# Moving three bias-broadcast DMAs from SyncE's queue to ScalarE's queue

## The chip, the cores and the metric

The kernel runs on one core of one Trainium2 chip. The metric is the device time of one execution in microseconds; the median of the timed executions counts. Times inside the kernel come from one profiled execution and are counted from the start of its span.

## What is computed

The program is one layer of a hybrid decoder for 2048 tokens of width 1024. Half of the heads run a recurrent mixer (RWKV-7), the other half attend over three dilated patterns; then come an output projection, a layer norm, a mixture of 32 experts and a second layer norm. What matters here is cut from the reference:

```python
proj = h @ w_in[i]
r_in, k_in, v_in, q_at, k_at, v_at = jnp.split(proj, splits, axis=-1)
y_rwkv = rwkv7_mix(h, r_in, k_in, v_in, ...)     # normalises k per head, then a scan over tokens
# in each of the three dilated branches of attention:
bias = jnp.transpose(rel_bias[t5_bucket(np.clip(rel, 0, None) * dil)], (2, 0, 1))
logits = jnp.einsum('bdhnqc,bdhnkc->bdhnqk', qs, kb) * (HEAD_DIM ** -0.5) + bias[None, None, :, None]
logits = jnp.where(valid, logits, NEG_INF)
```

The bias of a logit depends only on the head and on the distance of query and key, so for each of eight heads and three patterns it is one row of 384 numbers (masked places included), which attention later reads shifted by one place from query to query.

## The kernel before, in words

The kernel runs as a chain of stages: `project` (all projections, with the weights split into two float32r parts and three matmuls for each product), `mixers` (recurrence and attention interleaved), `mix_out`, `route` and `ple`, `experts`, `finish`. Stages pass their results through scratch tensors in DRAM.

The change lies in the third part of `project` (lines 430 to 488). It computes the recurrent keys and the attention's values in 16 steps: an outer loop over four chunks `cc` of 128 key channels, an inner one over four token blocks `tb` of 512. One step does, in TensorE's order:

- `key`: 24 matmuls into one PSUM bank. ScalarE writes a scaled copy `sh` (line 285), VectorE joins it with a token-shifted part into `o` (line 287), and SyncE's queue stores `o` to `rkk` (line 290). ScalarE squares it into `sq` (line 458).
- `value`, twice: 24 matmuls each; ScalarE copies the bank to `ov` (line 452), and SyncE's queue stores it to `va` (line 453).
- `norm`, between the two values: one matmul, a square root, a reciprocal (line 466), and a store of `rn` to `rkk` on SyncE's queue (line 468).
- one step of the generator `attn_bias` (line 950).

`attn_bias` does for each of the three patterns `n`: load `hot`, `rel_bias` and `gone` on GpSimd's queue (the last into `br`, line 959), yield, one matmul, a subtraction into `br` on VectorE (line 963), and one DMA that writes each of the eight rows of `br` 128 times into the scratch tensor `biasrow` (line 964, 1536 KB). Three empty yields follow, so the DMA comes once in four steps: in the second step of each of the first three chunks. `br` has one buffer, so the load for the next pattern waits until the DMA has read it. Attention reads `biasrow` only in the next stage.

Tiles are shared by tag. `sh`, `ov` and the attention part's `oh` all have tag "a" of the pool `st`, which has two buffers; `o` and others have tag "b" of the same pool. A step takes three tiles of tag "a" (`sh`, `ov`, `ov`), so `sh` of one step goes into the buffer that the first `ov` of the step before it had, and may be written only when that `ov` has been stored. Before ScalarE writes `sh`, VectorE puts one edge column into it (line 284). PSUM has five banks for the products of this stage.

The order on TensorE is the order of the program in `project` (a manual schedule). The order on the other engines is set at build time by the scheduler of the tile framework with a simulated timeline; at run time each engine and each engine's DMA queue runs its instructions in that order, each waiting for its own semaphores.

Of the kernel before, what the change touches and what calls it, by code (L numbers as in the profile page):

```python
# [18 lines left out]
P = 128  # L19
# [148 lines left out]
class K:  # L168
# [781 lines left out]
    def attn_bias(self, tile, bank):  # L950

        nc, I = self.nc, self.I
        L = 3 * P
        self.biasrow = rows = self.scratch("biasrow", (8, 3, P, L))
        for n in range(3):
            hot, br = tile(32, L + 8, "hot"), tile(8, L, "br")
            nc.gpsimd.dma_start(hot[:, 0:L], I["hot"][:, n])
            nc.gpsimd.dma_start(hot[:, L:], I["rel_bias"])
            nc.gpsimd.dma_start(br, I["gone"][:, n])
            yield  # L960
            ps = bank()
            nc.tensor.matmul(ps[0:8, 0:L], hot[:, L:], hot[:, 0:L], start=True, stop=True)
            nc.vector.tensor_tensor(out=br, in0=br, in1=ps[0:8, 0:L], op=ALU.subtract)
            nc.sync.dma_start(rows[:, n], br.unsqueeze(1).to_broadcast([8, P, L]))
            yield
            yield
            yield
# [1025 lines left out]
```

## Time and profile before

| | us |
|---|---|
| median of 3 timed runs | 3298.03 |
| lowest, highest | 3297.62, 3302.28 |
| profiled execution, device time | 3282.72 |
| its span | 3281.0 |
| the stage of keys and values, about | 345 to 610 |

| engine | busy us | share of the span |
|---|---|---|
| PE (TensorE) | 2936.9 | 90% |
| DVE (VectorE) | 2117.4 | 65% |
| ACT (ScalarE) | 1530.7 | 47% |
| POOL (GpSimd) | 675.9 | 21% |

DMA queue q1 is SyncE's (463.80 MB), q10 ScalarE's (20.14 MB) and q0 GpSimd's (45.93 MB). In a list of instructions in order of time a row gives start, duration, engine, line, operation, output<-input and how often; what stands in brackets is the idle time of the engine ahead of it and what ended that. SPq and ACTq rows are DMAs being issued by SyncE and ScalarE.

### The profile page before, as it was taken

How to read it: one execution, taken by the hardware profiler on the slowest of the kernel's cores; microseconds unless marked ns; L12 is line 12 of the kernel's file. 1: busy time of each engine (PE TensorE's matmuls, PEld its weight loads, DVE VectorE, ACT ScalarE, POOL GpSimd, SP SyncE). 2: the span in 40 equal slices, each digit the busy share in tenths (PEclk: the TensorE clock that was granted, in tenths of full speed). 3: DMA queues.
4: the chain of work that ended last, by engine and by line, in shares of the span. 5: the costliest groups of instructions: out<-in, count | busy, mean ns of one | idle time of the engine just before them, and what ended most of it. 6: DMA issues, size and time to landing. Idle time of an engine off the chain costs nothing. (4 is left out here: it accounts for less than half of the span.)

```text
span 3281.0 us, 49197 instructions
## 1 busy us (share of the span) xinstructions
PE 2936.9 (90%) x16686; PEld 2340.1 (71%) x16687; DVE 2117.4 (65%) x4730; ACT 1530.7 (47%) x3650; POOL 675.9 (21%) x682
## 2 busy tenths in 40 slices
PE   7989777999799999998998799899999999998880
PEld 6666666777587777877786577788777777776560
DVE  4997333687564766655756688653577877766756
ACT  3444211465354544543543233311477777765652
POOL 0442000244100211111202122323011111112216
PEclk9999888999899998998987899999999999999885
DMA  5213433588725326234204454233489999996845
GB/s 171 73 58 100 103 73 74 173 283 257 178 61 113 105 65 141 71 96 103 86 22 128 138 180 129 99 130 95 173 294 317 327 304 311 322 298 216 294 129 208
DMA packets 364063, 533.05 MB, mean 162 GB/s; under 512 B 92377, under 2 KB 204641, under 8 KB 363793
## 3 DMA queue, kind: packets, MB, share of 16 engines
q1 hardware_dynamic: 333240, 463.80, 45.3%
q0 software_dynamic: 14496, 45.93, 5.9%
q10 hardware_dynamic: 16072, 20.14, 1.9%
q8 instruction: 133, 2.18, 0.3%
q14 instruction: 122, 0.99, 0.1%
HBM read 402.27 MB, written 128.06 MB: 162 GB/s over the span
## 5 line engine op out<-in xcount | busy, mean ns | idle before, releaser
L1708 DVE TENSOR_TENSOR wl<-raw,wh 128x512 fp32r<-128x512 f32 x768 | 478.4, 683 | 91.1 <-ACT wh L1707 90.6
L1707 ACT CAST wh<-raw 128x512 fp32r<-128x512 f32 x768 | 418.1, 622 | 14.9 <-DMA raw<-in_w_up_dram 13.9
L198 PE MATMUL ps<-xh,wh 128*128 128x512 f32 x640 | 262.1, 410 | 1.0 <-ACT xh L322 1.0
L199 PE MATMUL ps<-xl,wh 128*128 128x512 f32 x640 | 258.5, 404 | 1.2 <-DVE xl L323 1.2
L200 PE MATMUL ps<-xh,wl 128*128 128x512 f32 x640 | 257.6, 403 | 0.0
L1085 ACT ACTIVATE pe<-pe,ms 128x256 f32<-128x256 f32 (+1 forms) x384 | 175.1, 458 | 142.2 <-DVE ms L1082 138.7
L1837 POOL DMA_INDIRECT acc<-ysb,ix x48 | 95.9, 1999 | 625.8 <-ACT ysb L1836 404.4
L198 PE MATMUL pe<-wh,XX 128*128 128x512 f32 x480 | 199.3, 415 | 3.8 <-ACT wh L1707 3.8
L199 PE MATMUL pe<-wl,XX 128*128 128x512 f32 x480 | 191.6, 399 | 2.3 <-DVE wl L1708 2.3
L200 PE MATMUL pe<-wh,XX 128*128 128x512 f32 x480 | 190.3, 396 | 0.0
L198 PEld LDWEIGHTS ps<-xh,wh 128*128 128x128 f32 x640 | 124.4, 194 | 34.5 <-issue 2.6
L199 PEld LDWEIGHTS ps<-xl,wh 128*128 128x128 f32 x640 | 124.3, 194 | 30.1 <-DVE xl L323 2.4
L200 PEld LDWEIGHTS ps<-xh,wl 128*128 128x128 f32 x640 | 124.0, 194 | 29.4
L1091 PE MATMUL pl<-eye,pe 128*128 128x128 f32 x600 | 126.5, 302 | 11.5 <-ACT pe L1085 11.0
L1066 PE MATMUL pl<-KK,Q 128*128 128x256 f32 x432 | 114.8, 392 | 16.5 <-DMA KK<-ks 16.2
L198 PE MATMUL pb<-gh,XH 128*128 128x512 f32 x320 | 126.6, 396 | 0.0
L199 PE MATMUL pb<-gl,XH 128*128 128x512 f32 x320 | 125.9, 393 | 0.0
L200 PE MATMUL pb<-gh,XL 128*128 128x512 f32 x320 | 125.4, 392 | 0.0
L1752 PE MATMUL pe<-wh,XX 128*128 128x512 f32 x288 | 119.7, 416 | 5.4 <-ACT wh L1707 5.4
L1105 PE MATMUL po<-pe,V 128*64 128x128 f32 x1200 | 119.9, 301 | 3.1 <-DVE O L1117 2.5
L1082 DVE CUSTOM_DVE_ANT_0 pe<-pl,bias 128x256 f32<-128x256 f32 x216 | 82.7, 418 | 60.8 <-PE pl L1066 42.5
L198 PE MATMUL pa<-woh,YH 128*128 128x512 f32 x256 | 110.7, 432 | 11.8 <-ACT YH L1335 11.8
(418 smaller groups left out, 7635.9 us busy)
## 6 DMA issues: line engine op xcount, KB each, us to landing
raw<-in_w_gate_dram SPq DMA_DIRECT2D x128, 512.0 KB
raw<-in_w_up_dram SPq DMA_DIRECT2D x128, 512.0 KB
raw<-in_w_down_dram SPq DMA_DIRECT2D x128, 512.0 KB
pk<-pk SPq DMA_DIRECT2D x32, 512.0 KB
pk_t<-pk SPq DMA_DIRECT2D x32, 512.0 KB
KK<-ks SPq DMA_DIRECT2D x64, 256.0 KB
wr<-in_w_in_dram SPq DMA_DIRECT2D x48, 256.0 KB
rkk<-rkk SPq DMA_DIRECT2D x32, 384.0 KB
```

The lines of the kernel that those rows point to most:

```text
L198: mm(out, lh, rh, start=first, stop=False)
L199: mm(out, lh, rl, start=False, stop=False)
L200: mm(out, ll, rh, start=False, stop=last)
L1066: mm(pl[:, h], q, toks(KK[:, m, h], n, prev, 2), start=m == 0, stop=m == 1)
L1082: nc.vector.tensor_tensor_reduce(out=pe[:, h, w], in0=pl[:, h, w], in1=add[:, h, w], scale=1.0, scalar=3e38, op0=ALU.add, op1=ALU.min, acc ...
L1085: nc.scalar.activation(pe[:, h, w], pe[:, h, w], AF.Exp, bias=m_[h], scale=-1.0, accum_out=s_[h])
L1091: nc.tensor.transpose(pt[:, h, b], pe[:, h, b * P:(b + 1) * P], self.c("eye"))
L1105: mm(o[h * 64:(h + 1) * 64, j], vb[:, h * 64:(h + 1) * 64], tt[:, h, b], start=b == kb[0], stop=b == 1)
L1707: nc.scalar.copy(wh[:, c], raw[:, c])
L1708: nc.vector.tensor_tensor(out=wl[:, c], in0=raw[:, c], in1=wh.bitcast(F32)[:, c], op=ALU.subtract)
L1752: mm(ps, L[:, 0:P], wh, start=first, stop=False)
L1837: nc.gpsimd.indirect_dma_start(out=self.acc, out_offset=bass.IndirectOffsetOnAxis(ap=ix[0:r, e, b:b + 1], axis=0), in_=ysb[0:r], in_offset ...
```

## The change

The DMA that writes the repeated rows of `br` to `biasrow` is issued by ScalarE instead of SyncE. Its bytes, its addresses and its place in the program's text stay as they are; it is issued three times.

```diff
             nc.vector.tensor_tensor(out=br, in0=br, in1=ps[0:8, 0:L], op=ALU.subtract)
-            nc.sync.dma_start(rows[:, n], br.unsqueeze(1).to_broadcast([8, P, L]))
+            nc.scalar.dma_start(rows[:, n], br.unsqueeze(1).to_broadcast([8, P, L]))
```

## Rows read from the trace of the kernel before

**Rows 1.** The page, busy tenths of TensorE in 40 slices of 82 us

```profile
PE   7989777999799999998998799899999999998880
```

**Rows 2.** Busy time by stretch: length, each engine's us (instructions), granted clock, DMA

```profile
398.00:402.00 4.00, 0.00 (x0) 0.00 (x0) 0.00 (x0) 0.00 (x0) 0.00 (x0) 0.50 0.45 51
410.00:414.00 4.00, 4.00 (x19) 3.73 (x18) 2.79 (x2) 0.63 (x1) 0.00 (x0) 0.50 0.18 65
...
420.00:440.00 20.00, 20.00 (x130) 17.12 (x128) 9.30 (x10) 5.59 (x10) 0.00 (x0) 1.00 0.17 60
```

**Rows 3.** ScalarE in order of time: the squaring of line 458, once a step

```profile
363.48 0.72 ACT L458 ACTIVATE sq<-o,prm 128x512 f32<-128x512 f32 x1 [0.82 <-DVE o L287]
376.57 0.72 ACT L458 ACTIVATE sq<-o,prm 128x512 f32<-128x512 f32 x1 [0.82 <-DVE o L287]
...
407.63 0.72 ACT L458 ACTIVATE sq<-o,prm 128x512 f32<-128x512 f32 x1 [2.04 <-DVE o L287]
422.15 0.73 ACT L458 ACTIVATE sq<-o,prm 128x512 f32<-128x512 f32 x1 [0.82 <-DVE o L287]
...
574.46 0.72 ACT L458 ACTIVATE sq<-o,prm 128x512 f32<-128x512 f32 x1 [0.82 <-DVE o L287]
586.59 0.73 ACT L458 ACTIVATE sq<-o,prm 128x512 f32<-128x512 f32 x1 [0.82 <-DVE o L287]
599.57 0.72 ACT L458 ACTIVATE sq<-o,prm 128x512 f32<-128x512 f32 x1 [0.91 <-DVE o L287]
```

**Rows 4.** Who waited for whom, 300 to 700: total us, times, longest

```profile
POOL br L959 <- DMA biasrow<-br: 66.4, 2, 33.2
DVE sh L284 <- DMA va<-ov: 64.2, 3, 21.4
```

**Rows 5.** SyncE's queue in order of time, around the first broadcast

```profile
370.87 0.33 SPq L964 DMA_DIRECT2D biasrow<-br  x1
371.53 8.88 SPq L468 DMA_DIRECT2D rkk<-rn  x1
380.50 4.19 SPq L290 DMA_DIRECT2D rkk<-o  x1
384.79 8.63 SPq L453 DMA_DIRECT2D va<-ov  x2
```

**Rows 6.** DMA queues, 372 to 380: packets, MB, share of 16 engines

```profile
q1 hardware_dynamic: 266, 0.41, 44.8%
```

**Rows 7.** ScalarE in order of time: the copies that write tag "a"

```profile
375.06 0.69 ACT L285 ACTIVATE sh<-ps,prm 128x512 f32<-128x512 f32 x1 [6.15 <-PE ps L200]
...
377.91 0.37 ACT L452 COPY ov<-ps 128x256 f32<-128x256 f32 x1 [0.62 <-PE ps L200]
...
404.89 0.69 ACT L285 ACTIVATE sh<-ps,prm 128x512 f32<-128x512 f32 x1 [16.85 <-DMA va<-ov]
```

**Rows 8.** VectorE in order of time: the subtraction ahead of the first broadcast

```profile
370.31 0.53 DVE L963 TENSOR_TENSOR br<-br,ps 8x384 f32<-8x384 f32 x1
```

**Rows 9.** DMA queues, 18 to 20: x tiles loading on both queues

```profile
q10 hardware_dynamic: 115, 0.47, 58.2%
q1 hardware_dynamic: 103, 0.36, 45.0%
```

**Rows 10.** The tile br: landing of its own small load

```profile
DMA to landing us min/median/max: 1.8/1.8/1.8
```

**Rows 11.** DMA queues, 420 to 430, no broadcast in flight

```profile
q1 hardware_dynamic: 432, 0.52, 14.5%
```

**Rows 12.** ScalarE in order of time: a 548 KB issue, then its next instruction

```profile
16.17 0.62 ACTq L1251 DMA_DIRECT2D slotlist<-in_empty_dram  x1
16.84 0.59 ACT L322 CAST xh<-tp 128x512 fp32r<-128x512 f32 x1
```

**Rows 13.** ScalarE and SyncE in order of time, around 1816

```profile
1815.56 3.95 ACTq L1292 DMA_DIRECT2D rbias<-in_router_g_b_dram  x1
...
1816.22 1.08 SPq L1276 DMA_DIRECT2D acc<-xr  x1
```

## The prediction

> **What bounds the kernel now.** I began with the page. TensorE is busy nine tenths of most slices, so a gain counts only where TensorE stands still. Among the early slices, those from 328 to 574 us show seven tenths [rows 1], and the stage of keys and values, in which the three broadcasts are issued, lies there. The page's chain of what ended last reaches only the last few per cent of the span and says nothing of this stage.
>
> Next came busy time by stretch. From 420 to 440 TensorE works all 20 us at full clock; from 398 to 402 no engine does anything, and the DMA engines together show 0.45 at 51 GB/s [rows 2]. So the stage has two modes: bound by TensorE, or everybody waiting for one transfer. [...]
>
> Then the length of the steps, read from the one squaring that each step has [rows 3]. A step with nothing special takes 586.59 - 574.46 = 12.13 us. The step after the first broadcast takes 407.63 - 376.57 = 31.06, the one after that 422.15 - 407.63 = 14.52.
>
> The waits name the reason: VectorE waited three times, 64.2 us in total, to write the edge of `sh`, each time for a store of `ov` to land [rows 4]. `sh` takes over the buffer of an `ov` of the step before. That small store is behind the broadcast on SyncE's queue. The broadcast's own issue at 370.87 takes 0.33 us; the next three rows of that queue last 8.88, 4.19 and 8.63 (for two) [rows 5]. From 372 to 380 the queue moved 266 packets and 0.41 MB, some 1540 B each, the size of one row of `br`, at 44.8% of 16 engines [rows 6]: the broadcast alone, on about half of the engines, while stores with rows of 1 and 2 KB were waiting. GpSimd's wait for the broadcast to have read `br` was 33.2 us [rows 4], so it lands near 371 + 33 = 404, and at 404.89 ScalarE at last writes `sh`, after 16.85 us idle [rows 7]. The chain is: broadcast, stores queued behind it, `ov` buffers held, `sh` not written, PSUM banks full, TensorE still.
>
> **The change part by part.**
>
> *Removed:* the broadcast from SyncE's queue, three times. Twelve steps, from 363.48 to 574.46, hold all three disturbances: 210.98 us [rows 3]. Clean, a group of four steps would be 4 x 12.13, plus 0.96 for the bias matmul and what goes with it (376.57 - 363.48 = 13.09), plus 0.85 for the step in which a new weight chunk is cast (599.57 - 586.59 = 12.98) [rows 3]: 50.33 us, and 151.0 for three. The loss is 210.98 - 150.99 = 60.0 us, clock included, as both the 31.06 and the 14.52 are in it. Where the casts are hidden it is 62.5. When the stall goes, what is late next is TensorE itself, which fills its stretches in every clean step [rows 2]. Later stages take their data from this one and have nothing that ran ahead during the standstill, so I let the whole gain through.
>
> *Added:* three DMA issues on ScalarE, of 0.33 us each by SyncE's row [rows 5]. The instruction waits for the subtraction on VectorE, which runs from 370.31 to 370.84 [rows 8]. Behind it on ScalarE waits `sh` of the next step, which is due only at 375.06 after 6.15 us of idle time [rows 7]. So both wait and issue lie in idle time and cost nothing; without that cover it would be 3 x 0.33 = 1.0 us. No other DMA is issued by ScalarE in the stage. On SyncE's queue nothing waits for `br` any longer.
>
> *Moved:* the broadcast now runs beside the stores instead of ahead of them. The trace has no broadcast beside SyncE's stores, so I bound this. The nearest row with both queues loaded is from 18 to 20 us: q10 moved 115 packets and q1 103, in the same 2 us [rows 9]. The two queues alternate, about packet for packet. A broadcast packet takes 8 us x 16 x 0.448 / 266 = 0.22 us of an engine [rows 6]. A store of 128 rows over 16 engines has 8 packets for each, and gets 8 x 0.22 = 1.7 us longer. The first `ov` of the step is copied by 378.3, its store issued by 378.7; with 1.8 us to land (the small load's value, an estimate for this store) [rows 10] and the 1.7 it is there at 382.2, and `sh` wants its buffer at about 375.06 + 12.98 = 388.0 [rows 7]. Some 5.8 us are spare: lower bound 0, and 0 is what I take, as the alternation in rows 9 is the nearest thing seen. The upper bound is that SyncE's issues stay held as they are now; that is the second case below, 18 us.
>
> *The broadcast itself* gets slower by the stores it now shares with. A store packet takes 10 x 16 x 0.145 / 432 = 0.054 us of an engine [rows 11]. In 33 us some 11 stores of 8 packets and two weight loads of 32 fall on each engine, 152 x 0.054 = 8 us: the broadcast lands after some 41 us, `br` is loaded 2.3 us later, at 371.2 + 43.3 = 414.5, and the next subtraction comes at 370.31 + 50.33 = 420.6 [rows 8]. That leaves 6 us. VectorE, with everything queued on it, would wait if the broadcast took over 47 us. I cost it at nothing.
>
> *Sum.* The profiled execution took 3282.72 us (span 3281.0), 15.3 us under the median of the timed runs; 60.0 us of it should go, which is 3222.7 there and 3298.0 - 60.0 = 3238.0 for the median.
>
> **The rivals.**
>
> *The issues stay held (partial gain).* If both queues draw on one generator of descriptors, SyncE's rows after the broadcast keep their 8.88, 4.19 and 8.63 us though their data may then pass. The second `ov` store is issued by 393.4, lands with the 3.5 us above at 396.9, and the copy that needs its buffer wants it at 377.91 + 12.98 = 390.9: 6.0 us late, three times, 18 us. That gives 3256. Against it: while ScalarE's own issue was held 3.95 us at 1815.56, SyncE issued at 1816.22 in 1.08 us [rows 13].
>
> *No change.* The stall stays if the broadcast keeps its engines to itself until it is done, whoever issued it: the store lands near 404 as now, and the time stays at 3298. For it: the broadcast does keep half of the engines busy for the whole stretch [rows 2, 6]. Against it: the packets of two queues side by side [rows 9]. [...]
>
> *Slower: ScalarE is held by its own issue.* If ScalarE can't go on until the broadcast has drained, 33.2 us from 371.2 on, `sh` is written at 404.4 instead of 375.06: 29.3 us late, against 16.85 us now [rows 7], so 12.5 us more each time, 37 in all, and 3336. The point from which this decides is a hold of 375.06 + 16.85 - 371.2 = 20.7 us; the sum of SyncE's held rows, 21.7 us [rows 5], is about that. Against it: those rows are later DMA issues, the broadcast's own row is 0.33 us, and after its 548 KB issue ScalarE started a cast within 0.67 us [rows 12].
>
> **How the numbers follow.** Forecast, whole gain: 0.76, 3238.0, by itself 3228 to 3248 (62.5 instead of 60.0 below with some room for another order of instructions on the engines that the build orders; above, 3 us left in each group). Issues held: 0.11, 3256. No change: 0.07. Slower: 0.06. To hold 8 in 10 the range takes in the first two with a few us more: 3228 to 3260. A measurement of this kernel can tell about 0.2% (6.6 us) from no change; faster by more than that has 0.76 + 0.11 = 0.87, within it 0.07, slower 0.06.
>
> **What would show it.** Right: steps of 12.1 to 13.1 us throughout the stage; no wait of VectorE or ScalarE for `va`; q1 and q10 both moving packets behind each broadcast; rows of SyncE as short as the broadcast's own; TensorE's clock at 1.00 through the stage; GpSimd's wait for the broadcast near 41 us. Wrong: a stretch without TensorE near 390, with SyncE's rows still long (issues held), or with short rows and `va` still landing late (engines), or ScalarE idle behind its own issue; or a stall at the subtraction, because `br` came late. If this stage is 60 us shorter and the total isn't, the gain went in a later stage.

## The result and the profile after

The changed kernel takes 3277.57 us in the median against 3294.36 of the kernel before on the same chip: ratio 0.9941, 95% interval 0.9916 to 0.9966. That is faster by some 17 us, where 60 were forecast, and the time lies above the forecast range of 3228 to 3260. The order of instructions on every engine is the one of before, but for the three DMAs that changed queues, so the two traces can be laid side by side.

The span of the profiled execution went from 3281.0 to 3260.4 us, and the stage of keys and values holds nearly all of that. Its measure is the time from the first squaring of line 458 to the sixteenth, 15 steps. Before it is 599.57 - 351.30 = 248.3 us (the end in [rows 3]). After, ScalarE in order of time (start, duration, engine, line, operation; idle time ahead and its reason in brackets):

```profile
351.07 0.72 ACT L458 ACTIVATE sq<-o,prm 128x512 f32<-128x512 f32 x1 [0.82 <-DVE o L287]
...
376.33 0.72 ACT L458 ACTIVATE sq<-o,prm 128x512 f32<-128x512 f32 x1 [0.82 <-DVE o L287]
...
401.06 0.72 ACT L458 ACTIVATE sq<-o,prm 128x512 f32<-128x512 f32 x1 [2.04 <-DVE o L287]
...
415.64 0.72 ACT L458 ACTIVATE sq<-o,prm 128x512 f32<-128x512 f32 x1 [0.82 <-DVE o L287]
...
580.21 0.72 ACT L458 ACTIVATE sq<-o,prm 128x512 f32<-128x512 f32 x1 [0.91 <-DVE o L287]
```

580.21 - 351.07 = 229.1 us: 19.1 less than before, of the 20.6 by which the span is shorter. So no later stage takes the gain back. But the stall is still there. The step after the first broadcast lasts 401.06 - 376.33 = 24.73 instead of 31.06 us, the one behind it 14.58 instead of 14.52 [rows 3].

Who waited for whom from 300 to 620 us (total, times, longest), to lay beside [rows 4]:

```profile
POOL br L959 <- DMA biasrow<-br: 71.7, 2, 35.9
...
DVE sh L284 <- DMA va<-ov: 47.8, 6, 15.1
...
ACT sh L285 <- DMA va<-ov: 31.5, 3, 10.5
```

It is the same wait as before, for the store of `ov`, only shorter: VectorE's longest is 15.1 instead of 21.4 us, and ScalarE sits idle for 10.5 instead of 16.85 [rows 7]. The clock suffers as before: in the first full stretch of TensorE after it, from 402 to 406 us, the granted clock was 0.50, as it was from 410 to 414 in the kernel before [rows 2].

SyncE's queue after, to lay beside [rows 5] (the two `ov` issues apart):

```profile
371.30 0.32 SPq L468 DMA_DIRECT2D rkk<-rn  x1
376.32 0.32 SPq L290 DMA_DIRECT2D rkk<-o  x1
378.07 2.86 SPq L453 DMA_DIRECT2D va<-ov  x1
381.79 3.68 SPq L453 DMA_DIRECT2D va<-ov  x1
...
399.19 0.32 SPq L468 DMA_DIRECT2D rkk<-rn  x1
```

SyncE is nearly free now: `rn` and `o`, held for 8.88 and 4.19 us before, are issued in 0.32. The two `ov` issues are still held, 2.86 and 3.68 us, but both are through by 385.47, and the store of the first `ov` stands in its queue by 380.93. Yet `sh`, which needs only that store, is written here:

```profile
370.63 0.55 ACTq L964 DMA_DIRECT2D biasrow<-br  x1
374.82 0.69 ACT L285 ACTIVATE sh<-ps,prm 128x512 f32<-128x512 f32 x1 [6.15 <-PE ps L200]
...
398.33 0.69 ACT L285 ACTIVATE sh<-ps,prm 128x512 f32<-128x512 f32 x1 [10.52 <-DMA va<-ov]
```

The small store needed some 20 us from its issue at 378.07 to its landing, for which `sh` waited until 398.33. Where it was stuck, the DMA queues of four stretches show (packets, MB, share of 16 engines; q10 is ScalarE's queue, q1 SyncE's). From 371.3 to 373:

```profile
q10 hardware_dynamic: 55, 0.08, 39.6%
q1 hardware_dynamic: 72, 0.13, 20.0%
```

From 373 to 376, from 378 to 380 (two stretches, one line each), and from 386 to 390:

```profile
q10 hardware_dynamic: 99, 0.15, 44.5%
...
q10 hardware_dynamic: 66, 0.10, 44.5%
...
q10 hardware_dynamic: 112, 0.17, 36.4%
q1 hardware_dynamic: 172, 0.24, 18.0%
```

The store of `rn` has 128 rows of 2 KB. At once, 72 packets and 0.13 MB of q1 pass: 64 rows, half of the store, and eight packets under 512 B. This half, the free one below, is taken to run on the engines on which there is no broadcast, eight of them if `br`'s eight rows keep one engine each (44.5% of 16 are 7.1). (No view names the engine of a packet; this is an estimate from the counts and the sizes.) Then q1 has no line at all from 373 to 376 and from 378 to 380, though half of `rn` and then half of `o` are waiting. From 380 to 384, from 384 to 386, and q10 from 371 to 384:

```profile
q1 hardware_dynamic: 72, 0.07, 5.3%
...
q10 hardware_dynamic: 55, 0.08, 40.3%
q1 hardware_dynamic: 15, 0.03, 5.2%
...
q10 hardware_dynamic: 421, 0.65, 43.1%
```

The 72 until 384 are 64 rows of 1 KB, again with eight packets under 512 B: the free half of the first `ov`. The 15 behind them are rows of 2 KB, the first of the held half of `rn`. So the other eight engines let a store through only near 385, some 13.5 us after the broadcast began, when q10 had moved between 421 and 476 packets: 53 to 60 of the 128 of each engine. By the 99 packets from 373 to 376, one of eight engines passes one in 8 x 3 / 99 = 0.24 us. From there on both queues move. Between 394 and 398 it is about two packets of the broadcast for one of a store:

```profile
q10 hardware_dynamic: 126, 0.19, 41.9%
q1 hardware_dynamic: 67, 0.06, 5.3%
```

Over eight engines that is 0.48 us for a store's packet. The first `ov` is third in line behind `rn` and `o`, and three stores of 8 packets take 24 x 0.48 = 11.5 us: 385 + 11.5 = 396.5, and `sh` follows at 398.3. That the stores ahead of it cost this is read from the trace; no run takes the stores apart. The theory drawn from this, called FRONT below: on an engine that both queues share, a long piece of the broadcast passes before the first store does, then they alternate, and a store also pays for the stores ahead of it in its own queue.

### The profile page after: what moved, and what is told of

It is laid out like the page before. It is cut to its first block, busy times and chain, and to the rows that moved or that the text cites. A ratio compares the mean times of both kernels' runs of the same rounds, so it can differ in the third digit from the quotient of the medians.

```text
span 3260.4 us, 49197 instructions
## 1 busy us (share of the span) xinstructions
PE 2938.1 (90%) x16686; PEld 2343.0 (72%) x16687; DVE 2118.0 (65%) x4730; ACT 1529.3 (47%) x3650; POOL 675.4 (21%) x682
## 5 line engine op out<-in xcount | busy, mean ns | idle before, releaser
L1707 ACT CAST wh<-raw 128x512 fp32r<-128x512 f32 x768 | 417.3, 620 | 13.2 <-DMA raw<-in_w_up_dram 12.1
L199 PE MATMUL pe<-wl,XX 128*128 128x512 f32 x480 | 192.0, 400 | 2.6 <-DVE wl L1708 2.6
L1753 PE MATMUL pe<-wl,XX 128*128 128x512 f32 x288 | 118.8, 413 | 2.9 <-DVE wl L1708 2.9
```

The costliest lines, as they stand in the source:

```text
L199: mm(out, lh, rl, start=False, stop=False)
L1707: nc.scalar.copy(wh[:, c], raw[:, c])
L1753: mm(ps, L[:, 0:P], wl, start=False, stop=last)
```

## The experiments

Each is measured by the stage (first to sixteenth squaring) and, where it was timed, by its ratio to the kernel before on the same chip. A stage without any stall would be 15 x 12.13 + 3 x 0.96 + 4 x 0.85 = 188.2 us by the clean steps of [rows 3].

| kernel | broadcast | stage us | ratio, 95% interval |
|---|---|---|---|
| before | 1 x 128 copies, SyncE | 248.3 | 1 |
| after | 1 x 128, ScalarE | 229.1 | 0.9941, 0.9916 to 0.9966 |
| quarters_now | 4 x 32 at once, ScalarE | 241.2 | 0.9969, 0.9942 to 0.9995 |
| pair_now | 2 x 64 at once, ScalarE | 230.7 | 0.9956, 0.9917 to 0.9994 |
| halves_act | 2 x 64, two steps apart, ScalarE | 211.8 | 0.9896, 0.9862 to 0.9931 |
| quarters_act | 4 x 32, one in each step, ScalarE | 187.6 | 0.9809, 0.9787 to 0.9830 |
| quarters_sp | 4 x 32, one in each step, SyncE | 187.6 | 0.9817, 0.9767 to 0.9867 |
| wide_act | from 128 partitions, ScalarE | 188.0 | 0.9843, 0.9816 to 0.9870 |
| wide_sp | from 128 partitions, SyncE | 187.9 | 0.9808, 0.9758 to 0.9859 |
| gpsimd | 1 x 128, GpSimd | 249.1 | 0.9995, 0.9965 to 1.0025 |

**Pieces, spread over the steps.** The same bytes from the same eight partitions, so that less of the broadcast can stand ahead of a store. The place of each piece is held behind the copy of the second `ov` (`at_act`, set in another line, is that copy).

```diff
-            nc.scalar.dma_start(rows[:, n], br.unsqueeze(1).to_broadcast([8, P, L]))
-            yield
-            yield
-            yield
+            nc.scalar.dma_start(rows[:, n, 0:32], br.unsqueeze(1).to_broadcast([8, 32, L]))
+            for c in range(1, 4):
+                yield
+                with self.tc.issue_after(self.at_act.ins): nc.scalar.dma_start(rows[:, n, c * 32:c * 32 + 32], br.unsqueeze(1).to_broadcast([8, 32, L]))
```

> The same on ScalarE's queue in four DMAs of 32 copies, one in each step behind the copies of the two `ov`. FRONT: silences of 7.5 us, the first `ov` through at about 371.3 + 7.5 + 3 = 382 against 388.0: no stall, stage near 188 to 190, the total 60 us under before and 41 under the changed kernel: ratio to before 0.982. BUSY ENGINES: the same bytes on the same engines, stage near 229, ratio 0.994. Rival GIVEN BACK (a later stage absorbs what this one gains): stage near 188, but the total only as the changed kernel's, 0.994.

The steps of quarters_act around the first broadcast:

```profile
376.25 0.72 ACT L458 ACTIVATE sq<-o,prm 128x512 f32<-128x512 f32 x1 [0.82 <-DVE o L287]
...
389.24 0.72 ACT L458 ACTIVATE sq<-o,prm 128x512 f32<-128x512 f32 x1 [0.91 <-DVE o L287]
...
401.15 0.73 ACT L458 ACTIVATE sq<-o,prm 128x512 f32<-128x512 f32 x1 [0.82 <-DVE o L287]
```

12.99 and 11.91 us, where the changed kernel has 24.73 and 14.58. The stage is 187.6, 60.7 under before, and the median 3227.11 against 3291.28. The 60 us of the sum were real, and they reach the end of the program, so GIVEN BACK falls. BUSY ENGINES falls too: the bytes and the engines are the same, and the stall is gone. TensorE is busy for 193.52 of 195 us there, at the full clock:

```profile
345.00:540.00 195.00, 193.52 (x1163) 166.28 (x1161) 92.27 (x102) 48.82 (x88) 3.08 (x6) 1.00 0.45 103
```

The DMA queues of quarters_act from 373 to 376 and from 379 to 381 show the short front: q10 alone in the first, and after 32 x 0.24 = 7.7 us the held stores all at once.

```profile
q10 hardware_dynamic: 99, 0.15, 45.0%
...
q1 hardware_dynamic: 243, 0.35, 47.4%
q10 hardware_dynamic: 13, 0.01, 8.3%
```

Two halves, the second two steps later, are the step between (the lines taken out are those above):

```diff
+            nc.scalar.dma_start(rows[:, n, 0:64], br.unsqueeze(1).to_broadcast([8, 64, L]))
+            for c in range(1, 4):
+                yield
+                if c == 2:
+                    with self.tc.issue_after(self.at_act.ins): nc.scalar.dma_start(rows[:, n, 64:128], br.unsqueeze(1).to_broadcast([8, 64, L]))
```

> The changed kernel's broadcast in two DMAs of 64 copies on ScalarE's queue, the second two steps (24 us) after the first. FRONT: each half is one silence of 14 to 15 us on the shared engines (64 x 0.24 = 15.4), and then the stores find them free: three stores behind each other are through 3 us later, the first `ov` at about 371.3 + 15.4 + 3 = 389.7 against 388.0 wanted: 0 to 3 us late, six times; stage 188 to 206 (229.1 after the change). Rival BUSY ENGINES (no front; stores are slowed as long as broadcast packets are in flight, in proportion): each half costs half of what the whole costs now, the same sum, stage near 229.

211.8 us is 5.8 over the upper end expected. What the expectation missed are the copies to `ov`: in each group one of them waits 9.0 us, the one in the step behind the second half, while ScalarE stands idle for 2.2 us at most ahead of `sh`.

```profile
ACT ov L452 <- DMA va<-ov: 27.0, 3, 9.0
```

The silence is as in the changed kernel (q10 alone from 379 to 381), but then the stores find the engines nearly free: 335 packets of q1 from 386 to 390, where the changed kernel moves 172. The DMA queues of halves_act in these two stretches:

```profile
q10 hardware_dynamic: 68, 0.10, 45.9%
...
q1 hardware_dynamic: 335, 0.43, 30.5%
q10 hardware_dynamic: 52, 0.07, 17.8%
```

A half by itself costs (211.8 - 187.6) / 6 = 4.0 us, the whole broadcast (229.1 - 187.6) / 3 = 13.8. So of the 13.8 us that the changed kernel still loses each time, clock included, a first half alone accounts for about 4. The other 10 would then come from the second half, with which three stores in line had to alternate; this is a difference of stages, not a run of its own.

**Pieces at once.** What makes the front as long as it is?

```diff
-            nc.scalar.dma_start(rows[:, n], br.unsqueeze(1).to_broadcast([8, P, L]))
+            for c in range(0, P, 64): nc.scalar.dma_start(rows[:, n, c:c + 64], br.unsqueeze(1).to_broadcast([8, 64, L]))
```

> The broadcast in two DMAs of 64 copies, issued by ScalarE one right after the other. With one DMA of 128 the stores were silent on the shared engines for about 64 packets (14 us), with four DMAs of 32 at once for about 96 (22 us). If the front is a fixed 64 packets: silence 14 us, stage 229. If the engine stays with a queue as long as further descriptors have arrived there by the time it gets to them: the second DMA is there in full, silence 28 us, `sh` some 13 us later than in the changed kernel, stage 240 to 255. ScalarE's second issue may be held, up to the 4.5 us that the third and the fourth quarter were, which by itself costs up to 1 us in each group.

230.7 us, q10 alone from 379 to 381 and 167 packets of q1 from 386 to 390: the changed kernel's picture. From 371 to 385 q10 moved 441 packets, 55 on each engine, so a second DMA that was there in full (both issues took 0.91 us together) did not lengthen the front. The 64 and the 96 packets in this expectation are misreadings: the changed kernel's front has 53 to 60, and the 96 were not one front, as follows. Four DMAs of 32 (the same edit with 32 for 64):

> The broadcast of the changed kernel, cut into four DMAs of 32 copies, issued one right after the other by ScalarE. Measure: from the first squaring of the stage to the sixteenth (15 steps): 248.3 us before, 229.1 after the change, 188.2 if every step were clean. Theory FRONT (what an engine has accepted of the broadcast, some 60 packets, goes ahead of every store, then both queues alternate): the accepted packets count and not the DMA they belong to, so the silence of the stores on the shared engines stays about 14 us and the stage stays near 229. Rival FRONT-BY-DMA (an engine finishes one DMA, then turns to the other queue): silence 32 x 0.24 = 7.5 us, stores 7 us earlier, `sh` some 3 us late instead of 10.5, stage near 200. Rival HELD SCALARE: the later issues wait for room (SyncE's row behind a whole broadcast lasted 8.9 us), `sh` is late for that: 5 us each, stage 229 to 245.

HELD SCALARE is what came. ScalarE in order of time, the last two issues and what came after:

```profile
371.30 4.49 ACTq L964 DMA_DIRECT2D biasrow<-br  x1
...
375.82 4.50 ACTq L964 DMA_DIRECT2D biasrow<-br  x1
...
380.45 0.69 ACT L285 ACTIVATE sh<-ps,prm 128x512 f32<-128x512 f32 x1 [12.06 <-DMA biasrow<-br]
```

The third and the fourth issue were held 4.5 us each, and `sh` was written at 380.45, 5.9 us late: the step lasts 18.99 us instead of 13.09 (17.34 and 17.27 in the other two groups). So ScalarE can indeed be held by its own DMAs. The three delays make 14.4 us, the stage is 12.1 longer than in the changed kernel, and 241.2 lies in the 229 to 245 of this rival.

The next `sh` was late as well, as in the changed kernel (ScalarE idle for 7.9 us behind `va`). But the silence was not of one piece. The DMA queues from 371 to 382, from 382 to 386, from 387 to 390 (q10 alone) and from 393 to 396:

```profile
q10 hardware_dynamic: 366, 0.55, 44.4%
q1 hardware_dynamic: 72, 0.13, 3.1%
...
q10 hardware_dynamic: 115, 0.18, 37.9%
q1 hardware_dynamic: 142, 0.26, 19.1%
...
q10 hardware_dynamic: 101, 0.15, 44.5%
...
q10 hardware_dynamic: 90, 0.13, 38.3%
q1 hardware_dynamic: 60, 0.11, 10.6%
```

Until 382 only the free half of `rn` has passed, while q10 moved 366 packets, 46 on each engine. From 382 to 386 q1 moves 0.26 MB, 128 rows of 2 KB: the held half of `rn` and the free half of `o`, issued at 381.95. Then the held half of `o` waits in its turn, until some 392.7. So `rn` and `o` were held for about 11 us each, one after the other, and FRONT, with a single front and then alternation, does not describe this run. What sets the length of a front, and why a second one follows here and not in the changed kernel, is left open.

**Another source.** The broadcast from 128 partitions, meant to spread it over more engines: its queue's share of the 16 came out at 79.3%, where the changed kernel has 44.5%. Cut: `br` has 128 partitions and `gone` is loaded to all of them, and `biasrow` is laid out as (3, 8, ...) instead of (8, 3, ...), with attention's read of it to match.

```diff
-            nc.tensor.matmul(ps[0:8, 0:L], hot[:, L:], hot[:, 0:L], start=True, stop=True)
-            nc.vector.tensor_tensor(out=br, in0=br, in1=ps[0:8, 0:L], op=ALU.subtract)
-            nc.scalar.dma_start(rows[:, n], br.unsqueeze(1).to_broadcast([8, P, L]))
+            nc.vector.tensor_copy(wide.rearrange("b (h t) -> b h t", t=16), hot[:, L:].unsqueeze(2).to_broadcast([32, 8, 16])); nc.tensor.matmul(ps[:, 0:L], wide, hot[:, 0:L], start=True, stop=True)
+            nc.vector.tensor_tensor(out=br, in0=br, in1=ps[:, 0:L], op=ALU.subtract)
+            nc.scalar.dma_start(rows[n].rearrange("h (t c) l -> (h t) c l", t=16), br.unsqueeze(1).to_broadcast([P, 8, L]))
```

> The broadcast leaves 128 partitions instead of 8: VectorE spreads the table's eight columns to 128, the matmul writes the bias row of a head to 16 partitions, `gone` is loaded to all 128, and each partition is written 8 times; still one DMA of 1536 KB on ScalarE's queue. FRONT: 64 packets for each of 16 engines, at the 0.054 to 0.1 us that a store's packet takes, are through in 4 to 7 us: no stall, stage near 189 (two small VectorE operations more), ratio 0.982. Rival MEMORY (the writing into DRAM limits the broadcast, at 51 GB/s): it takes 30 us on all 16 engines, no engine is left for the stores, and the stage is at or above the 248 of before.

188.0 us, no stall. The waits of wide_act have one line left on the broadcast, 7.6 us where it was 35.9:

```profile
POOL br L959 <- DMA biasrow<-br: 15.2, 2, 7.6
```

From 374 to 379 its queues moved 1.43 MB of the broadcast, 286 GB/s against 51 from eight partitions, and 144 packets of stores passed in the same stretch:

```profile
q10 hardware_dynamic: 934, 1.43, 79.3%
q1 hardware_dynamic: 144, 0.26, 14.4%
```

So DRAM takes the same bytes more than five times as fast, and MEMORY falls. A packet of 1536 B took 5 x 16 x 0.793 / 934 = 0.068 us of an engine, against 0.22 from eight partitions, and the share of the 16 engines was 79.3% against 44.5%. Three things changed together: the partitions read, the number of engines, and the order of `biasrow` in DRAM. Which of them shortened the packet is not shown. The total is 53 us under before, wide_sp's with the same stage 61; the intervals of their ratios overlap.

**Does the queue matter at all?** Both short forms on SyncE's queue, where the broadcast was before the change (the edits above with `nc.sync`; the later quarters stand behind the stores of `ov`):

> The four quarter broadcasts, one in each step behind the two stores of `ov`, on SyncE's queue as in the kernel before. If the length of what stands ahead of a store decides (the quarters on ScalarE's queue brought the stage to 187.6 us and the total to 0.981 of before), the queue hardly matters any more: a store waits at most 32 x 0.24 = 7.7 us, SyncE's issues aren't held, and stage and total come out as on ScalarE's queue: 188 to 190, ratio 0.981. Rival QUEUE (it is the sharing between two queues that brings the gain): behind each quarter all stores stand still on one queue, the stage stays 10 us or more above 188.

> The broadcast from 128 partitions, on SyncE's queue. GpSimd's wait for it on ScalarE's queue was 7.6 us, so stores that stand behind it wait about 6 to 8 us: no stall, stage about 188, ratio 0.984 as on ScalarE's queue. Rival QUEUE: `ov` late by some us in each group of four steps, stage 195 or more.

187.6 and 187.9 us, with ratios of 0.9817 and 0.9808: the same as on ScalarE's queue, within the intervals. SyncE's queue in quarters_sp:

```profile
370.84 0.33 SPq L964 DMA_DIRECT2D biasrow<-br  x1
371.50 0.35 SPq L468 DMA_DIRECT2D rkk<-rn  x1
376.54 0.32 SPq L290 DMA_DIRECT2D rkk<-o  x1
378.28 4.04 SPq L453 DMA_DIRECT2D va<-ov  x2
```

Behind a piece of 32 copies `rn` and `o` are not held, and the two `ov` stores take together little more than the time between their copies, 4.04 us. The rival QUEUE falls. All of the gain is to be had without a change of queue.

The third queue, with the broadcast whole:

```diff
-            nc.scalar.dma_start(rows[:, n], br.unsqueeze(1).to_broadcast([8, P, L]))
+            nc.gpsimd.dma_start(rows[:, n], br.unsqueeze(1).to_broadcast([8, P, L]))
```

> The whole broadcast of the changed kernel (8 partitions, 128 copies, one DMA), issued by GpSimd, which has nothing to do in this stage. The eight engines are the same kind of bottleneck. If a front of about 64 packets and then alternation is how any two queues share: stage near 229, as on ScalarE's queue. [...]

249.1 us and ratio 0.9995: as before the change, and not the 229 of a front and alternation. The DMA queues of gpsimd from 387 to 390 and from 391 to 396:

```profile
q0 software_dynamic: 34, 0.16, 49.1%
...
q0 software_dynamic: 49, 0.23, 41.6%
q1 hardware_dynamic: 51, 0.10, 6.6%
```

Packets of q0 carry 0.16 MB / 34 = 4.7 KB here, three rows each, and between 391 and 396 one store packet passed for each of them. No store packet passes from 387 to 390: the silence lasts some 5 us longer than on ScalarE's queue. A second queue by itself therefore promises nothing (19.1 us of the stage on ScalarE's, none on GpSimd's); it depends on what the second queue lets through, and when.

## Why the prediction was wrong

*What bounds the kernel* was read right: broadcast, store of `ov`, `sh`, PSUM, TensorE. With the stall gone the stage is 60.7 us shorter (60.0 in the sum), the total by 64 us in the median of quarters_act, and nothing later gives it back.

*Removed* and *added* were right. The subtraction, ScalarE's issue (0.55 us) and `sh` at 374.82 fit together as the forecast had it: the idle time ahead of `sh` is 6.15 us before and after. SyncE's rows for `rn` and `o` are short again; the two `ov` issues are held, 2.86 and 3.68 us instead of the 0.32 of the others, but off the path: the first is through at 380.93, before the shared engines let any store pass.

*Moved* is the step that failed: "The two queues alternate, about packet for packet", and from it 1.7 us for a store. Three things were wrong with it. First, the row it rested on [rows 9] shows two transfers that were both under way; nothing in it says how the second one gets in. Here the stores got in only after 53 to 60 broadcast packets of each engine, some 13.5 us. Secondly, the store was costed alone. Its own queue had `rn` and `o` ahead of it on the same engines, so it paid for 24 packets, not 8. Thirdly, a packet cost 0.48 us and not 0.22. Together the store landed near 398 instead of 382, and `sh` was 10.5 us late instead of 5.8 us early. The bound was no better than the value: its 18 us came from the issues being held. For the engines themselves only the two ends were priced, "packet for packet" (no loss) and "not at all" (the rival of no change, 3298, with a chance of 0.07), and the stage ended between them, with 229.1 - 187.6 = 41.5 us of loss left. A range that took in both ends would have reached 3298.

No run shows what sets the length of a front. Those here were 53 to 60 rows of 1536 B on an engine in the changed kernel, 55 in pair_now and 46 in quarters_now, and the alternation after the front is much finer, two packets of the broadcast for one of a store from 394 to 398.

*The broadcast itself:* 41 us were estimated for it, GpSimd's wait is 35.9, and the subtraction never waited for `br`. That margin was there.

*The rivals.* "Issues stay held" fell by SyncE's rows, of which only the two `ov` are still held, without effect on the first; the gain was partial, but for another reason than that one. "No change" is what happened on GpSimd's queue, and its 3298 is nearer to the measured 3277.57 than the forecast of 3238.0. "ScalarE is held" did not occur with one DMA, as the rows had said, but did with four in a row, for 4 to 6 us.

## What to carry to other kernels

A small transfer that stood behind a large one was freed only in part by another queue here, where by the counts both used the same DMA engines (19 of 60 us with ScalarE's queue, nothing with GpSimd's): ask how much of the large one can pass ahead of it, and what stands ahead of it in its own queue. Cut the large transfer into pieces that are shorter than the slack of whoever waits, one in each step of the loop, or spread its source over all partitions; here either took away the whole stall, on either queue. And a row that shows two transfers sharing tells how they share when both are under way, not how the second gets in.

## What was unexpected of the hardware

The DMA that repeats rows of 1536 B from 8 partitions moved 51 GB/s at 0.45 of the 16 engines [rows 2]; in wide_act the same bytes from 128 partitions moved at 286 GB/s and 79.3%. The stores of this stage, 128 rows each, went in two halves: the free half of `rn` was done within 2 us of its issue (72 packets of q1 from 371.3 to 373), while the other half began only some 13 us later (15 packets from 384 to 386). ScalarE's issues passed in 0.91 us for two DMAs of 64 rows an engine (pair_now), while of four DMAs of 32 rows the third and the fourth were held 4.5 us each (quarters_now), and with them the activations behind.
